# Conditioning blocks of a two-block network on one core: from matmuls and column sums to dot products along turned weight rows on VectorE

## The chip, the core and the metric

The kernel runs on one core of a Trainium2 chip. The metric is device time in microseconds (us), the median of several runs. TensorE is PE in the views (its weight load is PEld), VectorE is DVE, ScalarE is ACT, GpSimd is POOL, SyncE is SP. A name with q (ACTq, SPq) is that engine's instruction queue, where it issues DMAs.

## What is computed

A network of two blocks on 256 tokens of 1024 channels, in float32. Only the first block is touched. Its two layers are conditioned by one vector `c`: six vectors of 1024 per layer (shift, scale and gate of the mixer, shift, scale and gate of the feed-forward), each the product of `silu(c)` with a 1024 x 1024 slice of `w_ada`.

```
def first_block(x, c, w_ada, b_ada, ...):
    sc = jax.nn.silu(c)
    for i in range(DEPTH):
        mod = sc @ w_ada[i] + b_ada[i]
        sh_m, sc_m, g_m, sh_f, sc_f, g_f = jnp.split(mod, 6, axis=-1)
        h = modulate(x, norm_mix[i], sh_m, sc_m)
        ...                       # layer 0: attention; layer 1: gated short convolution
        x = x + g_m[:, None, :] * y
        h = modulate(x, norm_ffn[i], sh_f, sc_f)
        x = x + g_f[:, None, :] * swiglu(h, w_gate_up[i], w_down[i])
    return x
```

The second block (a gated recurrence or stick-breaking attention, memory attention, and a mixture of experts, twice) follows on the same core.

## The kernel before, in words

Weights come in pieces ("units") of [128, 1024] float32, 512 KB each, loaded by SP in an order written out in `make_plan`, into a ring of 34 buffers (`tS`, `raw`, `hi`, `lo` all live there). A "dense" unit is split into two float32r parts before it is multiplied: `hi` by a cast, mostly on ACT (L493), `lo = raw - hi` on DVE (L474). The tokens are two tiles of 128, T0 and T1. Each dense unit is used by both tiles with three matmuls per 128 rows of weights, so 12 matmuls of 512 columns a unit (L439).

The order of instructions on every engine is fixed when the program is built: `Sched` interleaves the parts of the program (tile 0, tile 1, splitting of units, the conditioning `ada_task`) by its own estimates of when each can go on. On the chip each engine then takes its instructions strictly in that order.

A conditioning block (i, j), layer i, vector j, is eight units. j is 0 and 3 for the shifts, 1 and 4 for the scales, 2 and 5 for the gates. In the plan the units of (0, 2) and (0, 4) alternate with units of `qkv`, those of (0, 3) with the eight units of the attention's output weights `wo`, those of (0, 5), (1, 1), (1, 0) and (1, 2) with the first feed-forward, and so on. Before the change there are two ways to work them:

* the five blocks in `ADA_PE`, all of layer 0, are **streamed** through PE: for each half of 512 columns eight matmuls with `silu(c)` as weights (`cs`, 32 columns wide, tile `bk<-raw,cs`), a copy to SBUF, four transposes and a reduction, which leave the vector as columns, one value a partition, in `mcol`;
* the other seven are **summed on DVE** over their eight units, `dst = w * cs[:, k] + dst` (L485, tile `tS<-raw,cs,tS`). The sums over partitions are then made on PE: for shifts and scales by matmuls with a column of ones (`bk<-one,tS`), for gates by splitting the sums and two matmuls of 512 columns with a matrix of ones for each half.

A gate ends as one row, repeated over the partitions, that multiplies the mixer's or the feed-forward's output. Shifts and scales are used by `lhsT_task`: when a tile is normalized (`modnorm`: a square on ACT, L465, a power on POOL, L508, a multiplication on DVE, L479), its halves are transposed on PE, multiplied and shifted by ACT with columns of `mcol` (L471), and split by ACT and DVE. The feed-forward of layer 0 so begins only when `mod0_4` and `mod0_3` are there.

Of the kernel before, what the change touches and what calls it, by code (L numbers as in the profile page):

```python
# [9 lines left out]
F32R = mybir.dt.float32r  # L10
U8 = mybir.dt.uint8
AF = mybir.ActivationFunctionType
# [11 lines left out]
ADA_PE = ((0, 1), (0, 0), (0, 2), (0, 4), (0, 3))  # L24
# [6 lines left out]
# ---------------------------------------------------------------- host layout  # L31
# [28 lines left out]
class Plan:  # L60
    """The order in which pieces of the weights are loaded."""
# [87 lines left out]
def host_arrays(inp):  # L149
# [3 lines left out]
    for i in range(2):  # L153
        for j in range(6):
            w = np.ascontiguousarray(g["w_ada"][i][:, j * D:(j + 1) * D])
            u[f"ada{i}_{j}"] = _split_units(w) if (i, j) in ADA_PE else w.reshape(8, 128, 1024)
# [27 lines left out]
    rows = np.stack([rowsrc[s] for k, (s, i) in zip(plan.kind, plan.src) if k == "row"])  # L184
# [47 lines left out]
# ---------------------------------------------------------------- emission order  # L232
class Sched:
    """Interleaves the parts of the program by an estimate of when each can go on."""
# [54 lines left out]
class Body:  # L289
# [68 lines left out]
    # ---- estimates of when the vector and scalar engines are done  # L358
# [23 lines left out]
    # ---- small helpers  # L382
# [128 lines left out]
    # ---- weights  # L511
# [104 lines left out]
    # ---- pieces  # L616
    def setup(self):
# [30 lines left out]
        self.act(self.cs, self.vecs[:, V_C:V_C + 8], AF.Silu)  # L648

# [20 lines left out]
    def gate(self, i):  # L670
        """Until everything before piece i that is not of its own line has been taken."""
        if i < self.ids["qkv"][6] and not self.again:
            return 0.0
        prev = -1
        for j in range(i - 1, -1, -1):
            if self.plan.kind[j] == "dense":
                prev = j
                break
        return lambda: 0.0 if self.seen >= prev else math.inf

    def ada_task(self):
        for i in range(2):
            order = [(j, (b,)) for b in range(2) for j in (1, 0)] if i == 0 else [(1, (0, 1)), (0, (0, 1))]
            for j, halves in order + [(j, (0, 1)) for j in (2, 4, 3, 5)]:
                uid = self.ids[f"ada{i}_{j}"]
                gate = j in GATES
                onpe = (i, j) in ADA_PE
                dst = None
                if gate or not onpe:
                    yield [self.gate(uid[0]), self.rS(1)]  # L690
                    dst = self.tS()
                if gate:
                    self.nc.gpsimd.memset(dst, 0.0)
                    self.nc.gpsimd.dma_start(dst[0:1, :], self.bada_d[6 * i + j:6 * i + j + 1])
                    yield 4.0
                if not onpe:
                    for k in range(8):
                        yield [self.gate(uid[k]), self.unit(uid[k]), lambda: self.tD - 0.8]
                        w = self.take(uid[k])
                        if k or gate:  # L700
                            self.stt(dst, w, self.cs[:, k:k + 1], dst, ALU.mult, ALU.add)
                        else:
                            self.ts(dst, w, self.cs[:, k:k + 1], None, ALU.mult, None)
                        self.done(uid[k])
                for b in halves:
                    d = dst[:, b * 512:(b + 1) * 512] if dst is not None else None
                    if onpe:
                        yield [self.gate(uid[4 * b + 3]), self.unit(uid[4 * b + 3]), self.bk(1)] + ([] if gate else [self.rH(1)])
                        bank = self.bank()
                        for q in range(4):  # L710
                            raw = self.take(uid[4 * b + q]).rearrange("p (k n) -> p k n", k=2)
                            for kk in range(2):
                                k = 2 * q + kk
                                gq = k % 4
                                self.mm(bank[32 * gq:32 * gq + 32], self.cs[:, k:k + 1].to_broadcast([128, 32]), raw[:, kk], k < 4, k >= 4)
                                self.sch.now -= 0.22
                            self.done(uid[4 * b + q])
                        if gate:
                            self.tt(d, bank, d, ALU.add)
                        else:  # L720
                            d = self.tH()
                            self.scopy(d, bank)
                        self.free()
                    if gate:
                        yield [self.rH(3)]
                        hi, lo = self.tH(F32R), self.tH(F32R)
                        ones = self.ones
                        if onpe:
                            ones = self.tH(F32R)[:, :128]
                            self.vcopy(ones, self.sel4[:, 0:1].to_broadcast([128, 128]))  # L730
                        self.split(hi, lo, d)
                        yield [self.w(), self.bk(1)]
                        bank = self.bank()
                        self.mm(bank, ones, hi, True, False)
                        self.mm(bank, ones, lo, False, True)
                        self.fH(3 if onpe else 2)
                        self.scopy(d, bank)
                    else:
                        yield [self.w(), self.bk(1)]
                        bank = self.bank()  # L740
                        m = self.mcol[:, i, j, 4 * b:4 * b + 4]
                        c = V_BA + 48 * i + 8 * j + 4 * b
                        if onpe:
                            for q in range(4):
                                self.tr(bank[:, q * 128:(q + 1) * 128], d[:, q * 128:(q + 1) * 128])
                            self.fH()
                            self.red(m, bank.rearrange("p (q g e) -> p q g e", q=4, e=32)[:, :, :, 0], ALU.add)
                            self.tt(m, m, self.vecs[:, c:c + 4], ALU.add)
                        else:
                            for q in range(4):  # L750
                                self.mm(bank[:, q:q + 1], d[:, q * 128:(q + 1) * 128], self.one, True, True)
                                self.sch.now += 0.1
                            self.tt(m, bank[:, :4], self.vecs[:, c:c + 4], ALU.add)
                        if j in (1, 4):
                            c = V_NG + 16 * i + (8 if j == 4 else 0) + 4 * b
                            self.stt(m, m, 1.0, self.vecs[:, c:c + 4], ALU.add, ALU.mult)
                        self.sch.ev[f"mod{i}_{j}_{b}"] = self.chain + 0.12
                    self.free()
                if gate:
                    self.mod[i, j] = dst  # L760
                    self.set(f"mod{i}_{j}")
                elif dst is not None:
                    self.fS()
# [1442 lines left out]
```

## Time and profile before

| | |
|---|---|
| median of 3 runs | 1243.78 us (1238.99 to 1245.82) |
| profiled execution, span from first to last instruction | 1241.5 us |
| PE busy in the span | 1185.2 us (95%) |
| DVE busy | 735.7 us (59%) |
| ACT busy | 548.4 us (44%) |
| bytes moved | 301.87 MB, mean 243 GB/s |

The time of the profiled execution outside its span is not given; the median is 2.3 us above the span. Busy time is an average over stages: the last of DVE's conditioning sums starts 655.5 us after the span's start, and everything that is changed lies before it or in the stage that uses it.

### The profile page before, as it was taken

Reading aid. Unit: us, or ns where it says so; the run is one execution under the profiler, and the core shown is the slowest. Engines: PE = TensorE matmul, PEld = TensorE weight load, DVE = VectorE, ACT = ScalarE, POOL = GpSimd, SP = SyncE. Lnnn points to the kernel's source line nnn. Section 1 sums busy time; section 2 is a strip of 40 time slices with the busy share of each in tenths; the row PEclk is TensorE's granted clock in tenths of the full one; section 3 lists DMA queues with packets and bytes.
Section 4 is the critical chain, followed back from the end, with each engine's and each line's share of the span. In section 5 each row is a group of like instructions: output and inputs, shape, how many; then the busy total and the mean of one; then the engine's idle time right before and its main releaser. Section 6 shows DMA issues by size and latency. Waiting matters only on the chain. (4 is left out here: it accounts for less than half of the span.)

```text
span 1241.5 us, 15838 instructions
## 1 busy us (share of the span) xinstructions
PE 1185.2 (95%) x5892; PEld 874.0 (70%) x5892; DVE 735.7 (59%) x1177; ACT 548.4 (44%) x912; POOL 45.2 (4%) x60
## 2 busy tenths in 40 slices
PE   7999999999989999999999999989998999899995
PEld 5777778888867887888887798765443786675432
DVE  4477667766768886555657567773313755564213
ACT  4565564534455556433445845422211566422211
POOL 0021000000000000000000001000000100000001
PEclk9999999999999999999999999989999899889998
DMA  9986768677766765556663323857999332487991
GB/s 378 408 283 231 277 219 294 243 260 268 278 229 234 278 228 174 211 208 208 209 211 106 118 86 125 313 206 279 394 408 360 139 133 101 156 325 288 410 409 42
DMA packets 83540, 301.87 MB, mean 243 GB/s; under 512 B 9408, under 2 KB 9824, under 8 KB 83456
## 3 DMA queue, kind: packets, MB, share of 16 engines
q1 hardware_dynamic: 82224, 298.39, 65.9%
q0 software_dynamic: 944, 2.02, 0.5%
q8 instruction: 48, 0.79, 0.3%
q10 hardware_dynamic: 288, 0.38, 0.1%
q14 instruction: 36, 0.29, 0.1%
HBM read 299.05 MB, written 2.10 MB: 243 GB/s over the span
## 5 line engine op out<-in xcount | busy, mean ns | idle before, releaser
L439 PE MATMUL bk<-hi,tS 128*128 128x512 f32 (+1 forms) x1760 | 585.8, 399 | 13.0 <-ACT hi L493 9.4
L439 PEld LDWEIGHTS bk<-hi,tS 128*128 128x128 f32 x1760 | 332.7, 190 | 88.9 <-ACT hi L493 10.0
L474 DVE TENSOR_TENSOR lo<-raw,hi 128x1024 fp32r<-128x1024 f32 x266 | 316.3, 1220 | 54.3 <-ACT hi L493 53.1
L439 PE MATMUL bk<-lo,tS 128*128 128x512 f32 (+1 forms) x880 | 344.5, 391 | 1.8 <-DVE lo L474 1.8
L493 ACT CAST hi<-raw 128x1024 fp32r<-128x1024 f32 x262 | 262.8, 1048 | 6.6 <-DMA raw<-in_units_dram 6.4
L439 PEld LDWEIGHTS bk<-lo,tS 128*128 128x128 f32 x880 | 167.5, 190 | 34.7 <-DVE lo L474 3.1
L467 ACT ACTIVATE tH<-bk 128x256 f32<-128x256 f32 (+1 forms) x94 | 42.2, 451 | 237.2 <-PE bk L439 237.1
L439 PE MATMUL bk<-hi,tH 128*128 128x512 f32 x384 | 132.8, 396 | 0.0
L439 PE MATMUL bk<-raw,tB 128*64 128x512 f32 x384 | 87.0, 602 | 0.0
L439 PEld LDWEIGHTS bk<-hi,tH 128*128 128x128 f32 x384 | 72.5, 189 | 15.0 <-issue 0.2
L474 DVE TENSOR_TENSOR tS<-bk,tS 128x512 fp32r<-128x512 f32 (+2 forms) x58 | 35.9, 633 | 70.2 <-ACT tS L493 68.9
L439 PE MATMUL bk<-raw,tH 128*64 128x512 f32 x320 | 74.5, 597 | 1.2 <-ACT tH L493 1.2
L439 PE MATMUL bk<-lo,tH 128*128 128x512 f32 x192 | 75.0, 391 | 0.0
L493 ACT CAST tS<-bk 128x512 fp32r<-128x512 f32 (+1 forms) x60 | 31.8, 544 | 92.3 <-PE bk L439 72.5
L485 DVE SCALAR_TENSOR_TENSOR tS<-raw,cs,tS 128x1024 f32<-128x1024 f32 x52 | 66.5, 1278 | 0.2
L439 PE MATMUL bk<-tS 128*128 128x256 f32 (+2 forms) x316 | 62.3, 342 | 0.0
L439 PEld LDWEIGHTS bk<-raw,tB 128*64 128x64 f32 x384 | 26.4, 138 | 49.3 <-issue 46.1
L439 PEld LDWEIGHTS bk<-tS 128*128 128x128 f32 x316 | 50.3, 203 | 11.2 <-issue 6.5
L474 DVE TENSOR_TENSOR tH<-tH,bk 128x256 f32<-128x256 f32 x44 | 18.4, 419 | 63.3 <-ACT tH L467 63.2
L451 PE MATMUL bk<-identr,tH 128*128 128x128 f32 x272 | 47.3, 279 | 8.5 <-DVE tH L474 5.9
L451 PEld LDWEIGHTS bk<-identr,tH 128*128 128x128 f32 x272 | 33.8, 141 | 30.3 <-issue 10.5
L493 ACT CAST tH<-bk 128x256 fp32r<-128x256 f32 (+1 forms) x52 | 18.5, 355 | 79.6 <-PE bk L451 75.5
(189 smaller groups left out, 1037.2 us busy)
## 6 DMA issues: line engine op xcount, KB each, us to landing
raw<-in_units_dram SPq DMA_DIRECT2D x556, 512.0 KB, 5.6
row<-in_rows_dram SPq DMA_DIRECT2D x9, 512.0 KB, 6.4
x<-in_x_dram SPq DMA_DIRECT2D x2, 512.0 KB, 8.8
xsave<-x POOLq DMA_DIRECT2D x2, 512.0 KB, 9.1
out_dram<-x SPq DMA_DIRECT2D x3, 256.0 KB, 2.0
ulv<-in_ulv_dram POOLq DMA_DIRECT2D x1, 576.0 KB, 7.2
cst<-in_consts_dram SPq DMA_DIRECT2D x1, 290.0 KB, 9.7
out_dram<-x ACTq DMA_DIRECT2D x1, 256.0 KB, 2.0
```

The lines of the kernel that those rows point to most:

```text
L439: self.nc.tensor.matmul(out, lhsT, rhs, start=start, stop=stop, skip_group_check=shared)
L451: self.nc.tensor.transpose(out, in_, self.ident)
L467: self.nc.scalar.activation(out, in_, func, scale=scale)
L474: self.nc.vector.tensor_tensor(out, a, b, op)
L485: self.nc.vector.scalar_tensor_tensor(out, a, s, b, op0, op1)
L493: self.nc.scalar.copy(out, a)
```

## The change

Three blocks of layer 0, the first shift, scale and gate, stay streamed. The blocks (0, 4) and (0, 3), and all that DVE summed before, are now **dot products**: the host turns the weights, so that a unit holds 128 output channels as rows, and one instruction on DVE multiplies a unit by `silu(c)`, repeated on every partition (`crow`), and adds along the row into one column of `mcol`. No sum over partitions is left. Gates become rows by eight transposes of the columns. `crow` is loaded and passed through Silu in `setup`.

```
-ADA_PE = ((0, 1), (0, 0), (0, 2), (0, 4), (0, 3))
+ADA_PE = ((0, 1), (0, 0), (0, 2))
...
-            u[f"ada{i}_{j}"] = _split_units(w) if (i, j) in ADA_PE else w.reshape(8, 128, 1024)
+            u[f"ada{i}_{j}"] = _split_units(w) if (i, j) in ADA_PE else np.ascontiguousarray(w.T).reshape(8, 128, 1024)
...
         self.act(self.cs, self.vecs[:, V_C:V_C + 8], AF.Silu)
+        self.crow = self.tS()
+        r = self.rows_d[self.rows_d.shape[0] - 1]
+        nc.scalar.dma_start(self.crow, bass.AP(tensor=r.tensor, offset=r.offset, ap=[[0, 128], [1, 1024]]))
+        self.act(self.crow, self.crow, AF.Silu)
...
+                if (i, j) in ADA_PE:
+                    yield from self.ada_streamed(i, j, halves, uid)
+                else:
+                    yield from self.ada_dots(i, j, uid)
+        self.fS()
...
+    def ada_dots(self, i, j, uid):
+        for b in range(2):
+            for q in range(4 * b, 4 * b + 4):
+                yield [self.gate(uid[q]), self.unit(uid[q]), lambda: self.tD - 0.8]
+                w = self.take(uid[q])
+                self.nc.vector.scalar_tensor_tensor(w, w, 1.0, self.crow, ALU.mult, ALU.mult,
+                                                    accum_out=self.mcol[:, i, j, q:q + 1])
+                self.onD(1024)
+                self.chain = self.tD = self.tD + 0.1
+                self.done(uid[q])
+            self.ada_column(i, j, b)
+            if j not in GATES:
+                self.sch.ev[f"mod{i}_{j}_{b}"] = self.chain + 0.12
+        if j in GATES:
+            yield [self.w(), self.rS(1)]
+            dst = self.tS()
+            for b in range(2):
+                yield self.bk(1)
+                bank = self.bank()
+                for q in range(4):
+                    k = 4 * b + q
+                    self.tr(bank[:, q * 128:(q + 1) * 128], self.mcol[:, i, j, k:k + 1].to_broadcast([128, 128]))
+                self.scopy(dst[:, b * 512:(b + 1) * 512], bank)
+                self.free()
```

`ada_column` adds the bias (and for scales the gain), as before. `ada_streamed` is the old code for the streamed blocks.

**The start, on ACT.** First before the change, then after; `vecs` holds `c` by columns, and `tS<-in_rows` is the load of `crow`.

```order
L626 DMA vecs<-in_vecs_dram 128x234
L457 ACT_TABLE_LOAD
L467 ACTIVATE cs<-vecs 128x8 [waits DMAHW0_49]
L493 CAST tS<-raw 128x1024 [waits DMAHW1_49]
L493 CAST hi<-raw 128x1024 [waits DMAHW2_49]
```

```order
L626 DMA vecs<-in_vecs_dram 128x234
L457 ACT_TABLE_LOAD
L467 ACTIVATE cs<-vecs 128x8 [waits DMAHW0_49]
L651 DMA tS<-in_rows_dram 128x1024
L467 ACTIVATE tS<-tS 128x1024 [waits DMAHW1_49]
L493 CAST tS<-raw 128x1024 [waits DMAHW2_49]
L493 CAST hi<-raw 128x1024 [waits DMAHW3_49]
```

The load of `crow` is issued by ACT behind the wait for `vecs`, and its Silu, which waits for that load, stands ahead of the first casts of weights.

**The turn from the attention's output weights to the feed-forward, on DVE.** `x_82` and `x_83` are the two tiles, L479 is their normalization, and `tS<-tS 128x512` the split of a normalized half. Before the change:

```order
L474 TENSOR_TENSOR tH<-bk,tS 128x512
L474 TENSOR_TENSOR x_83<-x_83,tH 128x512
L474 TENSOR_TENSOR lo<-raw,hi 128x1024 x2
L474 TENSOR_TENSOR tH<-tH,bk 128x256
L481 TENSOR_SCALAR tm<-tm 128x1
L479 TENSOR_SCALAR tS<-x_83,tm 128x1024
L474 TENSOR_TENSOR tH<-bk,tH 128x256
L485 SCALAR_TENSOR_TENSOR tS<-raw,cs,tS 128x1024
L474 TENSOR_TENSOR tS<-tS 128x512 x2
```

After it (L711 are the dots; here they are of block (0, 3)):

```order
L479 TENSOR_SCALAR tS<-x_82,tm 128x1024
L474 TENSOR_TENSOR lo<-raw,hi 128x1024
L481 TENSOR_SCALAR tm<-tm 128x1
L479 TENSOR_SCALAR tS<-x_83,tm 128x1024
L711 SCALAR_TENSOR_TENSOR raw,mcol<-raw,tS 128x1024 x3
L474 TENSOR_TENSOR mcol<-mcol,vecs 128x4
L711 SCALAR_TENSOR_TENSOR raw,mcol<-raw,tS 128x1024
L474 TENSOR_TENSOR tS<-tS 128x512 x2
L711 SCALAR_TENSOR_TENSOR raw,mcol<-raw,tS 128x1024
L474 TENSOR_TENSOR lo<-raw,hi 128x1024 x2
L711 SCALAR_TENSOR_TENSOR raw,mcol<-raw,tS 128x1024 x2
L474 TENSOR_TENSOR mcol<-mcol,vecs 128x4
```

Seven of the eight dots of (0, 3) now stand behind the normalization of both tiles. Before the change nothing of this block was left there, and T0 had been normalized and split 11 rows of DVE ahead of T1.

**The first feed-forward, on PE.** `identr,tH` are the two transposes of a tile's activations, `hi,tH` and `lo,tH` the matmuls with its down weights, `hi,tS` and `lo,tS` those of the gate and up weights. Before, from one of the eleven steps:

```order
L451 MATMUL bk<-identr,tH 128x128 x2
L439 MATMUL bk<-hi,tS 128x512
L439 MATMUL bk<-lo,tS 128x512
L439 MATMUL bk<-hi,tS 128x512 x2
L439 MATMUL bk<-lo,tS 128x512
```

After:

```order
L451 MATMUL bk<-identr,tH 128x128 x2
L439 MATMUL bk<-hi,tH 128x512
L439 MATMUL bk<-lo,tH 128x512
L439 MATMUL bk<-hi,tH 128x512 x2
L439 MATMUL bk<-lo,tH 128x512
L439 MATMUL bk<-hi,tH 128x512
L451 MATMUL bk<-identr,tH 128x128 x2
```

Both tiles now go through the steps side by side; in nine of the eleven the down matmuls of T0 follow right on its own transposes, where twelve or more matmuls of other work stood between.

## Rows read from the trace of the kernel before

**Rows 1.** Page, part 1: engine, busy us (share of the span), instructions.

```profile
PE 1185.2 (95%) x5892; PEld 874.0 (70%) x5892; DVE 735.7 (59%) x1177; ACT 548.4 (44%) x912; POOL 45.2 (4%) x60
```

**Rows 2.** Stretches: PE, PEld, DVE, ACT, POOL busy us (instructions); clock; DMA.

```profile
103.40:154.80 51.40, 51.40 (x316) 38.74 (x315) 35.81 (x61) 27.78 (x54) 5.87 (x5) 1.00 0.73 260
171.50:176.50 5.00, 2.20 (x11) 1.81 (x11) 3.95 (x7) 2.25 (x6) 0.57 (x1) 0.79 0.32 114
180.00:340.00 160.00, 160.00 (x738) 132.06 (x737) 112.82 (x129) 69.71 (x98) 1.50 (x2) 1.00 0.76 266
372.00:465.00 93.00, 89.54 (x427) 73.56 (x426) 78.48 (x124) 50.48 (x79) 0.55 (x1) 1.00 0.70 248
```

**Rows 3.** Timeline of ACT from the start: start us, us, instruction, [idle before <-releaser].

```profile
4.85 0.21 ACT L467 ACTIVATE cs<-vecs 128x8 f32<-128x8 f32 x1 [2.39 <-DMA vecs<-in_vecs_dram]
4.97 1.03 ACT L493 CAST tS<-raw 128x1024 fp32r<-128x1024 f32 x1
...
12.58 1.04 ACT L493 CAST hi<-raw 128x1024 fp32r<-128x1024 f32 x1 [0.23 <-DMA raw<-in_units_dram]
```

**Rows 4.** DMA issues of the first 3 us: KB each, median us to landing.

```profile
vecs<-in_vecs_dram ACTq DMA_DIRECT2D x1, 117.0 KB, 4.1
```

**Rows 5.** Timeline of PE from the start, with a streamed half.

```profile
7.09 0.79 PE L439 MATMUL bk<-hi,tS 128*128 128x512 f32 x1 [7.09 <-ACT hi L493]
...
24.20 1.92 PE L439 MATMUL bk<-raw,cs 128*32 128x512 f32 x16
26.05 0.50 PE L439 MATMUL bk<-hi,tS 128*128 128x512 f32 x1
...
27.55 0.60 PE L451 MATMUL bk<-identr,tH 128*128 128x128 f32 x4
27.90 0.48 PE L439 MATMUL bk<-hi,tS 128*128 128x512 f32 x1
```

**Rows 6.** Timeline of PE at 262 to 268 us: half of a column sum.

```profile
263.87 0.95 PE L439 MATMUL bk<-one,tS 128*128 128x1 f32 x8
264.68 0.48 PE L439 MATMUL bk<-hi,tS 128*128 128x512 f32 x1
```

**Rows 7.** Groups by form: count, busy us, mean ns, idle before.

```profile
L485 DVE SCALAR_TENSOR_TENSOR tS<-raw,cs,tS 128x1024 f32<-128x1024 f32 x52 | 66.5, 1278 | 0.2
L485 DVE SCALAR_TENSOR_TENSOR tS<-x,tS 128x1024 fp32r<-128x1024 f32 x4 | 4.9, 1225 | 2.2 <-ACT tS L467 2.2
L469 ACT ACTIVATION_READ_ACCUMULATOR tH<-bk,tm 128x1 f32 x32 | 6.3, 197 | 0.0
```

**Rows 8.** Timeline of DVE, 100 to 180 us.

```profile
127.22 0.18 DVE L1039 RECIPROCAL tm<-tm 128x4 f32<-128x4 f32 x1 [1.63 <-ACT tH L469]
...
158.06 2.35 DVE L474 TENSOR_TENSOR lo<-raw,hi 128x1024 fp32r<-128x1024 f32 x2
...
169.00 0.69 DVE L474 TENSOR_TENSOR tH<-bk,tS 128x512 f32<-128x512 f32 x1 [1.45 <-PE bk L439]
...
174.02 0.75 DVE L479 TENSOR_SCALAR tS<-x,tm 128x1024 f32<-128x1024 f32 x1 [0.70 <-POOL tm L508]
```

**Rows 9.** Timeline of PE, 170 to 177 us.

```profile
174.92 1.94 PE L451 MATMUL bk<-identr,tS 128*128 128x128 f32 x8 [1.41 <-DVE tS L479]
176.51 0.78 PE L439 MATMUL bk<-hi,tH 128*128 128x512 f32 x1
```

**Rows 10.** Timeline of ACT at the same place.

```profile
176.04 1.50 ACT L471 ACTIVATE tS<-bk,mcol 128x128 f32<-128x128 f32 x4 [2.13 <-PE bk L451]
177.58 0.62 ACT L493 CAST tS<-tS 128x512 fp32r<-128x512 f32 x1
```

**Rows 11.** Timeline of all engines, 193.5 to 195.6 us, in the feed-forward.

```profile
193.82 0.38 PE L451 MATMUL bk<-identr,tH 128*128 128x128 f32 x2
...
194.24 0.37 ACT L493 CAST tH<-bk 128x256 fp32r<-128x256 f32 x1 [1.62 <-PE bk L451]
```

**Rows 12.** PE's waits, 410 to 500 us: total us, times, longest.

```profile
PE bk L439 <- ACT tS L493: 2.5, 2, 1.8
```

More of the change, by code (lines that the diff above doesn't have):

```diff
@@ L183, in host_arrays @@
     rowsrc["row_gn"] = np.concatenate([g["a_gnorm_2"][0], np.zeros(256, np.float32)])
-    rows = np.stack([rowsrc[s] for k, (s, i) in zip(plan.kind, plan.src) if k == "row"])
+    rows = np.stack([rowsrc[s] for k, (s, i) in zip(plan.kind, plan.src) if k == "row"] + [g["c"][0]])
     b_all = np.ascontiguousarray(g["b_ada"].reshape(12, 1024))
@@ L685, in ada_task @@
                 uid = self.ids[f"ada{i}_{j}"]
[L686 to L763, printed above, removed]
+                if (i, j) in ADA_PE:
[3 more added lines that the diff above has]
+        self.fS()
+    def ada_column(self, i, j, b):
+        m = self.mcol[:, i, j, 4 * b:4 * b + 4]
+        c = V_BA + 48 * i + 8 * j + 4 * b
+        self.tt(m, m, self.vecs[:, c:c + 4], ALU.add)
+        if j in (1, 4):
+            c = V_NG + 16 * i + (8 if j == 4 else 0) + 4 * b
+            self.stt(m, m, 1.0, self.vecs[:, c:c + 4], ALU.add, ALU.mult)
@@ new lines, in ada_dots @@
+    def ada_dots(self, i, j, uid):
[22 more added lines that the diff above has]
+                self.free()
+            self.mod[i, j] = dst
+            self.set(f"mod{i}_{j}")
@@ new lines, in ada_streamed @@
+    def ada_streamed(self, i, j, halves, uid):
+        gate = j in GATES
+        dst = None
+        if gate:
+            yield [self.gate(uid[0]), self.rS(1)]
+            dst = self.tS()
+            self.nc.gpsimd.memset(dst, 0.0)
+            self.nc.gpsimd.dma_start(dst[0:1, :], self.bada_d[6 * i + j:6 * i + j + 1])
+            yield 4.0
+        for b in halves:
+            d = dst[:, b * 512:(b + 1) * 512] if gate else None
+            yield [self.gate(uid[4 * b + 3]), self.unit(uid[4 * b + 3]), self.bk(1)] + ([] if gate else [self.rH(1)])
+            bank = self.bank()
+            for q in range(4):
+                raw = self.take(uid[4 * b + q]).rearrange("p (k n) -> p k n", k=2)
+                for kk in range(2):
+                    k = 2 * q + kk
+                    gq = k % 4
+                    self.mm(bank[32 * gq:32 * gq + 32], self.cs[:, k:k + 1].to_broadcast([128, 32]), raw[:, kk], k < 4, k >= 4)
+                    self.sch.now -= 0.22
+                self.done(uid[4 * b + q])
+            if gate:
+                self.tt(d, bank, d, ALU.add)
+            else:
+                d = self.tH()
+                self.scopy(d, bank)
+            self.free()
+            if gate:
+                yield [self.rH(3)]
+                hi, lo = self.tH(F32R), self.tH(F32R)
+                ones = self.tH(F32R)[:, :128]
+                self.vcopy(ones, self.sel4[:, 0:1].to_broadcast([128, 128]))
+                self.split(hi, lo, d)
+                yield [self.w(), self.bk(1)]
+                bank = self.bank()
+                self.mm(bank, ones, hi, True, False)
+                self.mm(bank, ones, lo, False, True)
+                self.fH(3)
+                self.scopy(d, bank)
+            else:
+                yield [self.w(), self.bk(1)]
+                bank = self.bank()
+                for q in range(4):
+                    self.tr(bank[:, q * 128:(q + 1) * 128], d[:, q * 128:(q + 1) * 128])
+                self.fH()
+                self.red(self.mcol[:, i, j, 4 * b:4 * b + 4], bank.rearrange("p (q g e) -> p q g e", q=4, e=32)[:, :, :, 0], ALU.add)
+                self.ada_column(i, j, b)
+                self.sch.ev[f"mod{i}_{j}_{b}"] = self.chain + 0.12
+            self.free()
+        if gate:
+            self.mod[i, j] = dst
+            self.set(f"mod{i}_{j}")
```

## Prediction

> **What bounds the kernel now.** First the page's busy times: PE works in 95% of the span, DVE in 59%, ACT in 44% [rows 1]. The average hides stages, so next the busy time by stretches [rows 2]. In the attention (103.4 to 154.8 us) and in most of the first feed-forward (180 to 340 us) PE is busy for every microsecond, at a granted clock of 1.00, with DMA at 0.73 and 0.76 and DVE at 0.70 of the time. There a matmul taken from PE gives back its time, 160.00 us / 738 = 0.217 us, and work added to DVE is free as long as nobody waits for it. Two places are otherwise. At the turn from the output weights `wo` to the feed-forward (171.5 to 176.5) PE works 2.20 of 5.00 us: it waits for residual, norm and affine. In 372 to 465 us DVE is busy for 78.48 of 93 us, with little room. So the question is not how much DVE gets to do, but what stands behind it at the turn and at the start.
>
> **The change, term by term** (plus is longer).
>
> *The start, +6.0.* Before, ACT gets `vecs` at 4.85 and casts at once, at 4.97 [rows 3]; PE starts at 7.09, behind that work [rows 5]. After, ACT issues the 512 KB load of `crow` only at about 5.0, waits for it, and passes it through Silu, and all first casts are queued behind. The nearest row for the landing is `vecs`: 4.1 us for 117 KB, issued beside the same stream of weight loads [rows 4]. With some 0.9 us for four times the bytes it lands at 10.0; a Silu over 1024 columns costs about what the cast of 1024 does, 1.03 [rows 3]; so the first cast stands at 11.0 instead of 4.97, and PE begins at 13.1. The lower bound is +5 (landing as `vecs` did, 9.1). The upper one is +9 to +10: if the load came in only behind the seven weight loads issued by then, the last of which releases ACT at 12.58 [rows 3], the first cast would be at 13.9. I take the lower half, since `vecs` itself was issued among those loads and was not held back to their end. Nothing gives this back: PE has no gap until 154.8.
>
> The Trainium skill (DMA: Bandwidth & Descriptors, section "Queues, rings and completion order") says that a DMA engine takes turns between the queues it has work for, packet by packet. By that rule ACT's load shares with SP's and the term is +6; by plain order it would be +10. The 4.1 us agree with the rule.
>
> *Streaming of (0, 4) and (0, 3), -9.* A half has a group of matmuls with `cs` from 24.20 to 26.05, 1.85 us, and four transposes from 27.55 to 27.90, 0.35 us [rows 5]: 2.2 us. Four halves are 8.8, with the transposes' own start-up (2.45 a half) 9.8. All lay where PE was full.
>
> *Column sums, -6.5.* Eight matmuls of one column take from 263.87 to 264.68, 0.81 us [rows 6], once for each of the eight halves of (1, 1), (1, 0), (1, 4), (1, 3). Four lie in the full stretch (-3.2 sure); the others lie near the DVE-heavy one, where they may give nothing. That is put into the term for the second layer below.
>
> *Gates of layer 0's feed-forward and layer 1, 0.* Four matmuls of 512 columns (0.9 us) go, eight transposes (0.8 us before they overlap) come.
>
> *One dot, 1.3 us.* No row has a multiplication with a sum along the row on DVE. Nearest: the same instruction without a sum, from two SBUF operands, at 1278 and 1225 ns [rows 7]; ACT's reading of an accumulator costs 197 ns as a separate instruction [rows 7]. So 1.2 to 1.5; I take 1.3. Before, 52 of the same length and four shorter ones were there; now 72. The 16 more that come from the streamed blocks, some 21 us of DVE, stand between 100 and 185 us.
>
> *DVE behind PE in the attention, +1.7.* In 103.4 to 154.8 DVE worked 35.81 us [rows 2], and waited for exponentials as at 127.22 (1.63) [rows 8], four times, some 5 us in all. Three dots join it before the last attention split of T1: 35.8 + 3.9 + 5 = 44.7, while PE without streaming needs 51.4 - 9 = 42.4. Between 0 (the waits shrink when DVE comes later) and +2.5; I take 1.7.
>
> *The turn, +15.7, the largest.* Seven of the eight dots of (0, 3) stand behind the norm of both tiles, and no matmul of the feed-forward can go before them, since ACT adds the shift. Counting from PE's last `wo` matmul: residual of T1 1.3 (twice 0.69, as at 169.00), a `lo` of 1.15 (2.35 for two, at 158.06), T0's norm with its wait for POOL 1.5 (0.70 + 0.75, at 174.02) [rows 8], another `lo` 1.15, T1's norm 1.5, three dots 3.9, the bias 0.2, ACT's affine 1.5 and cast 0.6 [rows 10], and 0.2 between engines: 13.0 us. PE has only eight transposes to do, which cost it 0.8 net; 12.2 idle. If the POOL waits are hidden, 10.8. The second half: a dot, two tile splits (0.7 each, paced by ACT's casts), a dot, two `lo`, two dots, a bias, about 11.5 with its waits, then affine and cast of both tiles, 2.3: 13.8, against 24 matmuls (5.2), transposes and what is left of PE's earlier work (3.1): 5.5 idle. Then the first Silu and the transposes of both tiles, now side by side, 2.0. Together 19.7 us in place of what stands there now: 1.41 before the transposes at 174.92 and the rest up to 176.51 [rows 9], with the 2.13 for which ACT waits at 176.04 [rows 10] inside it, about 4. Now T0's matmuls cover T1's norm; after it both tiles wait for the same dots. The term is +15.7, from +11 (second half fully covered, POOL hidden) to +18.
>
> *The feed-forward side by side, +6.* In nine of eleven steps T0's down matmuls follow on its own transposes. Row: transposes at 193.82, ACT's cast at 194.24 for 0.37, so `hi` is there at 194.61 [rows 11]; 0.8 us after the start, of which the transposes occupy 0.15. 0.65 x 9 = 5.9. It is 0 if DVE and ACT are ahead by then; they are not likely to be, as the cast waits for the transposes themselves.
>
> *Second layer, -2.5.* Now PE waits twice for a cast, 2.5 us in all, on entering the second feed-forward [rows 12]; after, T1 still has matmuls of the mixer left there. Against it stand the column sums' doubtful 3.2. Bounds -3 to +3.
>
> Sum: 6.0 - 9 - 6.5 + 1.7 + 15.7 + 5.9 - 2.5 = +11.3. The profiled span is 1241.5; the median of the runs shown is 1243.8, 2.3 above, and carries over: 1252.8 of span, some 1254.5 of median (rounded down by half a microsecond, since more bounds lie below a term than above).
>
> **Rivals.** *The costs are half hidden, no measurable change.* The waits at the turn are at their lower bound (+11), the lockstep costs 2 instead of 6, the start 5: 5 - 9.5 - 6.5 + 1 + 11 + 2 - 2.5 = +0.5, about 1244. For it: ACT and DVE do have room on average. Against it: the three dots ahead of the first affine stand in a fixed order, and nothing for PE stands beside them.
>
> *Faster: the turn is covered.* One mechanism: PE reaches the end of `wo` later than DVE's queue allows, so that the dots run while `wo` is still multiplied, and the turn costs what it does now. Then 6 - 9 - 6.5 = -9.5, about 1234. It decides when the extra idle at the turn and behind it is under 9.5 us. For it: the units come in early (DMA at 0.73). Against it: the dots stand behind T1's norm, and that behind the last `wo` matmul.
>
> *Dots at half speed.* The nearest row without a sum, 1278 ns, twice, is 2.56 us a dot. Six dots on the path at the turn add 7.7, and some 16 dots in the stretch with 14.5 us of DVE left (372 to 465) add 20 - 14.5 = 6 to 20. About 1254.5 + 7.7 + 13 = 1275. For it no row; against it that the two operands from SBUF alone do not cost double in 1278 ns.
>
> The Trainium skill (Vector Engine (DVE) Microarchitecture Reference, section "7. Points that are easy to get wrong") says that this form with two sources in SBUF that are not bf16 halves its throughput, as no port is left for the accumulator. The rows without accumulator show 1024 elements in 1278 ns; none here shows the form with one.
>
> *The load of `crow` comes last.* The start at +10: 1258.5, inside the forecast's own range.
>
> **How the numbers follow.** The forecast, 1248 to 1262 with its own bounds, has 0.55 (with the late `crow`); half hidden 0.25; the covered turn 0.14; slow dots 0.06. A change of 0.5%, 6.2 us, is about what a measurement can tell here from none. Below 1237.6: most of the covered turn and little else, 0.15. Within: the half-hidden case and the lower edge of the forecast, 0.27. Above 1250: 0.58. The range leaves out the slow dots and the lower half of the covered turn: 1236 to 1267.
>
> **What would show it.** In the changed profile: PE's first matmul at about 13 us; a PE gap of some 12 us ahead of the feed-forward's first matmuls, released by ACT's affine, with three dots and no waits ahead of it on DVE, and a second of some 5; dots at 1.2 to 1.5 us each; small gaps of 0.6 us released by ACT's cast in the first feed-forward; no `one` matmuls. The forecast is wrong if the start is under 10 us, if PE idles less than 12 us in all at the turn, or if the steps run gapless.

## The result, and the profile after

The changed kernel takes 1271.53 us (median of 4 runs, 1270.74 to 1274.44) against 1243.01 us before: ratio 1.0236, 95% interval 1.0209 to 1.0264. It is slower, as forecast, but by 28.5 us where 11 were forecast, and outside the range. The profiled execution has a span of 1270.0 us.

The page's busy times after, beside [rows 1]:

```profile
PE 1178.0 (93%) x5760; PEld 869.3 (68%) x5760; DVE 749.9 (59%) x1261; ACT 545.9 (43%) x905; POOL 39.9 (3%) x54
```

PE's busy time is only 7 us less, not 15 (a matmul at the lower clock counts its longer time), and PE is idle for 92 us instead of 56. To find where, I count on PE's timeline the matmuls of 512 columns with `hi` or `lo` parts of weights, which are the same work in both kernels, and compare when the n-th starts (the first is n = 0). The difference to before, in us:

```
n      place                             before at   after   difference
0      start                                 7.1      15.5     +8.4
300    ahead of the attention              102.0     110.3     +8.4
475    near the end of wo                  164.9     166.9     +2.0
540    behind the turn                     185.4     204.2    +18.8
1200   late in the first feed-forward      344.5     365.9    +21.3
1500   second layer's mixer                431.1     448.1    +17.0
1740   second feed-forward                 495.1     521.0    +25.9
2520   start of the second block           683.6     711.1    +27.6
```

Where the kernels' orders differ, the n-th matmul need not be the same one, so a single row can be off; at the end the difference is 28.5 us. Four places lose: the start, the turn, the entry into the second feed-forward, and a little, 2.6 us, behind n = 1740. Two stretches gain: the attention, where streaming is gone, and the way to the second layer's mixer, where the column sums and some older waits are.

**The start.** ACT's timeline (start, us, instruction, idle before), to be read against [rows 3]:

```profile
5.31 0.21 ACT L467 ACTIVATE cs<-vecs 128x8 f32<-128x8 f32 x1 [2.84 <-DMA vecs<-in_vecs_dram]
...
12.52 1.06 ACT L467 ACTIVATE tS<-tS 128x1024 f32<-128x1024 f32 x1 [7.01 <-DMA tS<-in_rows_dram]
13.49 1.03 ACT L493 CAST tS<-raw 128x1024 fp32r<-128x1024 f32 x1
```

The load of `crow`, issued at 5.31, holds ACT for 7.01 us; the first cast stands at 13.49 instead of 4.97. By the trace's landing times the load was there at 12.50, ahead of two weight loads issued before it (13.06 and 14.32), so the rival that it comes last is out. PE's first row follows:

```profile
15.51 0.79 PE L439 MATMUL bk<-hi,tS 128*128 128x512 f32 x1 [15.51 <-ACT hi L493]
```

**The turn.** PE's timeline from the last `wo` matmul, where before there were the waits of [rows 9]:

```profile
167.81 0.39 PE L439 MATMUL bk<-hi,tS 128*128 128x512 f32 x1
173.52 1.11 PE L451 MATMUL bk<-identr,tS 128*128 128x128 f32 x4 [5.32 <-DVE tS L479]
176.30 1.08 PE L451 MATMUL bk<-identr,tS 128*128 128x128 f32 x4 [1.67 <-DVE tS L479]
182.09 0.79 PE L439 MATMUL bk<-hi,tS 128*128 128x512 f32 x1 [4.70 <-ACT tS L493]
182.68 0.63 PE L439 MATMUL bk<-lo,tS 128*128 128x512 f32 x1
...
193.03 0.80 PE L439 MATMUL bk<-hi,tS 128*128 128x512 f32 x1 [2.57 <-ACT tS L493]
```

The four waits are 14.3 us: two for the norms of T0 and T1, one for the dots with the affine, one for the second half. DVE at the same place, with both norms (L479) ahead of the dots:

```profile
172.71 0.75 DVE L479 TENSOR_SCALAR tS<-x,tm 128x1024 f32<-128x1024 f32 x1 [0.75 <-POOL tm L508]
...
175.40 0.75 DVE L479 TENSOR_SCALAR tS<-x,tm 128x1024 f32<-128x1024 f32 x1 [0.74 <-POOL tm L508]
176.07 1.22 DVE L711 SCALAR_TENSOR_TENSOR raw<-raw,tS 128x1024 f32<-128x1024 f32 x1
177.21 0.08 DVE L711 DVE_READ_ACCUMULATOR raw<-raw,tS 128x1 f32 x1
177.21 1.22 DVE L711 SCALAR_TENSOR_TENSOR raw<-raw,tS 128x1024 f32<-128x1024 f32 x1
```

Behind the waits the matmuls are slow at first. The stretches (PE, PEld, DVE, ACT, POOL busy; then the granted clock):

```profile
170.00:180.00 10.00, 2.20 (x8) 1.43 (x8) 8.44 (x16) 1.74 (x4) 1.13 (x2) 0.61 0.57 206
180.00:190.00 10.00, 7.91 (x30) 6.40 (x31) 7.49 (x11) 5.93 (x12) 0.00 (x0) 0.71 0.41 119
190.00:200.00 10.00, 7.43 (x29) 5.81 (x28) 5.82 (x10) 7.72 (x14) 0.00 (x0) 0.83 0.44 153
```

Eight matmuls from 182.09 to 185.66 take 3.57 us, at the lower of the two clock levels (1.2 instead of 2.4 GHz), where 8 x 0.217 = 1.74 was the pace of [rows 2].

**The dots**, in the groups by form and line:

```profile
L711 DVE SCALAR_TENSOR_TENSOR raw<-raw,tS 128x1024 f32<-128x1024 f32 x72 | 86.9, 1219 | 0.0
L711 DVE DVE_READ_ACCUMULATOR raw<-raw,tS 128x1 f32 x72 | 5.9, 83 | 0.0
```

**The steps of the first feed-forward.** One of nine equal rows on PE, the first matmul of T0's down weights:

```profile
218.61 0.50 PE L439 MATMUL bk<-hi,tH 128*128 128x512 f32 x1 [0.46 <-ACT tH L493]
```

**The entry into the second feed-forward.** PE, and below it DVE, at the end of the second layer's mixer:

```profile
477.66 0.39 PE L439 MATMUL bk<-hi,tS 128*128 128x512 f32 x1
484.19 1.97 PE L451 MATMUL bk<-identr,tS 128*128 128x128 f32 x8 [6.14 <-DVE tS L479]
```

```profile
475.13 4.62 DVE L474 TENSOR_TENSOR lo<-raw,hi 128x1024 fp32r<-128x1024 f32 x4
479.67 0.68 DVE L474 TENSOR_TENSOR tH<-bk,tS 128x512 f32<-128x512 f32 x1
480.39 0.69 DVE L474 TENSOR_TENSOR x<-x,tH 128x512 f32<-128x512 f32 x1
481.00 1.65 DVE L485 SCALAR_TENSOR_TENSOR tB<-tB,vecs 128x127 f32<-128x127 f32 x8
482.57 0.15 DVE L481 TENSOR_SCALAR tm<-tm 128x1 f32<-128x1 f32 x1
483.38 0.75 DVE L479 TENSOR_SCALAR tS<-x,tm 128x1024 f32<-128x1024 f32 x1 [0.66 <-POOL tm L508]
```

PE ends T0's output matmuls at 477.9 and has nothing else: T1's convolution is only being worked on (481.00, and again until 495). As at the turn, the eight matmuls behind the transposes are slow, 3.56 us from 485.81 on, with a granted clock of 0.53 from 484 to 490. Before, T1's output matmuls stood there, T0's transposes followed them without a wait, and the waits were those of [rows 12]:

```profile
469.48 0.39 PE L439 MATMUL bk<-hi,tS 128*128 128x512 f32 x1
469.71 1.04 PE L451 MATMUL bk<-identr,tS 128*128 128x128 f32 x8
472.55 0.50 PE L439 MATMUL bk<-hi,tS 128*128 128x512 f32 x1 [1.80 <-ACT tS L493]
```

### The profile page after: what moved, and what is told of

Same layout as the page of the kernel before. It is cut to its first block, busy times and chain, and to the rows that moved or that the text cites. A ratio compares the mean times of both kernels' runs of the same rounds, so it can differ in the third digit from the quotient of the medians.

```text
span 1270.0 us, 15613 instructions
## 1 busy us (share of the span) xinstructions
PE 1178.0 (93%) x5760; PEld 869.3 (68%) x5760; DVE 749.9 (59%) x1261; ACT 545.9 (43%) x905; POOL 39.9 (3%) x54
## 5 line engine op out<-in xcount | busy, mean ns | idle before, releaser
L474 DVE TENSOR_TENSOR lo<-raw,hi 128x1024 fp32r<-128x1024 f32 x266 | 316.8, 1222 | 65.4 <-ACT hi L493 64.3
L711 DVE SCALAR_TENSOR_TENSOR raw<-raw,tS 128x1024 f32<-128x1024 f32 x72 | 86.9, 1219 | 0.0
L451 PE MATMUL bk<-identr,tH 128*128 128x128 f32 x256 | 44.6, 277 | 11.2 <-DVE tH L474 4.4
L474 DVE TENSOR_TENSOR tH<-bk,tH 128x256 fp32r<-128x256 f32 (+1 forms) x52 | 20.8, 401 | 53.6 <-ACT tH L493 53.6
```

Source lines behind the costliest of these rows:

```text
L451: self.nc.tensor.transpose(out, in_, self.ident)
L474: self.nc.vector.tensor_tensor(out, a, b, op)
L711: self.nc.vector.scalar_tensor_tensor(w, w, 1.0, self.crow, ALU.mult, ALU.mult, accum_out=self.mcol[:, i, j, q:q + 1])
```

## The experiments

The theory after this reading: start, turn and second entry each cost what the table shows. The rivals: that the start is absorbed later; that the second entry only follows from the turn, or from DVE's load; that the turn's cost is the length of the dots, or the order of the tiles. Kernel n is the kernel of experiment n.

**1. `crow` off the start** (e1_crow_late): SP loads it beside `x[1]`.

```
-        nc.scalar.dma_start(self.crow, ...)
-        self.act(self.crow, self.crow, AF.Silu)
+        self.onA(1024)
...
+                self.nc.sync.dma_start(self.crow, ...)
...
+                if (i, j, halves) == (0, 1, (1,)):
+                    self.nc.scalar.activation(self.crow, self.crow, AF.Silu)
```

`onA` keeps the program's estimate of ACT's time as it was.

> The changed kernel with the load of crow issued by SP beside the load of the second tile of tokens, and its Silu on ACT behind the first streamed block instead of ahead of the first casts. If the 8.4 us by which PE starts later are carried to the end, 1271.5 - 8.4 = about 1263, with PE's first matmul near 7 us again. If they are absorbed at a later wait (the turn's dots were late in any case), 1270 to 1272.

Measured: 1264.99 us, ratio 1.0182 (1.0158 to 1.0207). The difference to the changed kernel's ratio is 0.54%, 6.7 us: most of the 8.4 is carried to the end.

**2. (0, 4) and (0, 3) streamed again, the rest dots** (e2_l0_streamed).

```
-ADA_PE = ((0, 1), (0, 0), (0, 2))
+ADA_PE = ((0, 1), (0, 0), (0, 2), (0, 4), (0, 3))
```

> The changed kernel with the blocks (0, 4) and (0, 3) streamed through PE again; (0, 5) and the second layer stay dots, crow stays at the start. If the loss on entering the second feed-forward is made by the second layer's own dots on a full DVE: +8.4 (start) - 6 (column sums) + 9 on 1243 = about 1254, with the wait of some 6 us before the second feed-forward still there. If that loss only follows from the tiles going side by side since the first turn: 1243 + 8.4 - 6 = about 1245, and the wait is gone. In both cases no wait above 2 us at the first turn.

Measured: 1255.5 us, ratio 1.0110 (1.0086 to 1.0135). The difference to before, counted as above, is +8.3 at the start, -1.0 at n = 1500 and +7.5 at n = 1740: everything gained on the way to the second layer is given back at the entry into the second feed-forward, with its wait:

```profile
467.16 1.97 PE L451 MATMUL bk<-identr,tS 128*128 128x128 f32 x8 [5.82 <-DVE tS L479]
```

The wait does not come from the first turn, which is untouched here.

**3. Only (0, 4) and (0, 3) as dots** (e3_l0_dots_only): the kernel before, with

```
+DOTS = ((0, 4), (0, 3))
...
+                if (i, j) in DOTS:
+                    yield from self.ada_dots(i, j, uid)
+                    continue
```

> The kernel before with only the blocks (0, 4) and (0, 3) as dots; (0, 5) and the second layer stay column sums on DVE, crow is at the start. If the second layer's loss is made by its own dots: start 8.4 + turn and lockstep 10 to 14 on 1243 = 1262 to 1266. If it follows from the tiles side by side: 1271 to 1277, with the wait before the second feed-forward there too.

Measured: 1270.69 us, ratio 1.0220 (1.0193 to 1.0246), between the two expectations. The time is nearly that of the changed kernel, but the loss is made up otherwise. The wait of 6 us ahead of the second feed-forward is not there (1.81 is the longest), and the second layer's column sums are not saved (+25.6 at n = 1200, +23.5 at n = 1500). The stretch behind them loses 6 us all the same (+29.4 at n = 1740), in shorter waits and at a lower clock (last section).

**4. The start alone** (e4_start_only): the kernel before with the four lines that make `crow`.

> The kernel before with nothing added but the load of crow and its Silu at the start. If the later start is carried: 1243 + 8.4 = about 1251. If it is absorbed in some later wait of PE: 1243 to 1245.

Measured: 1249.43 us, ratio 1.0059 (1.0036 to 1.0081), 7.3 us. The difference to before is +8.5 at the start and still +8.7 at n = 1740. The start is settled.

**5. Short dots in the second layer** (e5_short_l1_dots), on kernel 2:

```
+                n = 8 if (i, j) in ((1, 4), (1, 3)) else 1024
-                self.nc.vector.scalar_tensor_tensor(w, w, 1.0, self.crow, ...
+                self.nc.vector.scalar_tensor_tensor(w[:, :n], w[:, :n], 1.0, self.crow[:, :n], ...
```

> As e2_l0_streamed, but the 16 dots of (1, 4) and (1, 3) read only 8 of their 1024 columns (so these two vectors lack nearly all of their sum); the order of instructions is the same. It takes some 16 us of DVE out of the second layer's mixer. If DVE sets the entry into the second feed-forward and so gave back the 9 us that PE gained there: 1255.5 - 6 to -9 = 1246 to 1250, and the wait of 5.8 us shrinks to under 2. If the order of the tiles alone makes that wait: 1253 to 1256, with the wait above 4 us.

Measured: 1253.41 us, ratio 1.0084 (1.0061 to 1.0107); the wait is 5.81 us, unchanged. DVE's time on these dots doesn't make it.

**6. Short dots of (0, 3)** (e6_short_turn_dots): the changed kernel, with the same edit and `(i, j) == (0, 3)`.

> As the changed kernel, but the eight dots of (0, 3) read only 8 of their 1024 columns (so this shift lacks nearly all of its sum); the order is the same. If the length of the dots at the turn makes the turn dear: PE's waits of 4.7 and 2.6 us go to under 2.5 together, and with the clock behind them 1271.5 - 7 to -9 = 1263 to 1265. If it is the order (both norms uncovered): the waits of 5.3 and 1.7 us ahead of the transposes stay, and the time is 1268 to 1271.

Measured: 1268.55 us, ratio 1.0213 (1.0192 to 1.0235). The waits at the turn are 5.32, 1.67, 1.52 and 1.81, 4.0 less in sum, and the time is about 3 us lower (the intervals overlap): the dots' length at the turn is the smaller part of its cost.

**7. The units of (0, 3) loaded earlier** (e7_turn_early), on kernel 1:

```
-    weave([("qkv", "dense")] * 12, ada(0, 2) + ada(0, 4))
-    weave([("wo", "dense")] * 8, ada(0, 3))
+    weave([("qkv", "dense")] * 12, ada(0, 2) + ada(0, 4) + ada(0, 3))
+    put("wo", "dense", 8)
```

> As e1_crow_late, but the units of (0, 3) are loaded among those of qkv, ahead of wo, so that their dots lie before the turn. If the dots' place was the turn's cost: PE's idle time at the turn falls from 14 to about 7 us (both norms stay uncovered), 1265 - 7 to -9 = 1256 to 1258. If DVE or the loads become late in the attention instead: 1263 or more, with PE waits between 100 and 165 us above the 3.4 us of now.

Measured: 1268.72 us, ratio 1.0219 (1.0200 to 1.0238), above kernel 1. PE idles 14.7 us at the turn (4.31, 0.47, 7.66, 2.22) and 5.5 us in the attention. The edit moved the loads, but the dots did not come to lie before the turn. DVE behind T1's norm:

```profile
167.25 0.75 DVE L479 TENSOR_SCALAR tS<-x,tm 128x1024 f32<-128x1024 f32 x1 [0.74 <-POOL tm L508]
167.92 1.22 DVE L713 SCALAR_TENSOR_TENSOR raw<-raw,tS 128x1024 f32<-128x1024 f32 x1
...
169.46 1.22 DVE L713 SCALAR_TENSOR_TENSOR raw<-raw,tS 128x1024 f32<-128x1024 f32 x1
```

The last dot of (0, 4), at 167.92, and all eight of (0, 3), from 169.46 on, stand behind both norms, where kernel 1 has seven. So this run does not test the dots' place; it shows that loading the units earlier, in this order, buys nothing.

**8. Kernels 1 and 2 in one** (e8_late_streamed).

> e1_crow_late and e2_l0_streamed in one: crow off the start, (0, 4) and (0, 3) streamed, only (0, 5) and the second layer as dots. If the terms add up: 1255.5 - 7 = 1248 to 1249, still 4 to 7 above the kernel before, by the wait ahead of the second feed-forward and one at the entry to the second block. If the earlier start lets the second layer's units come in late: 1252 or more.

Measured: 1246.99 us, ratio 1.0040 (1.0025 to 1.0055). The terms add up, to within 1 us.

**9. The units of (1, 4) and (1, 3) earlier** (e9_l1_early), on kernel 8:

```
-    weave(ffn(0), ada(0, 5) + ada(1, 1) + ada(1, 0) + ada(1, 2))
-    weave([("win", "dense")] * 24, ada(1, 4) + ada(1, 3))
+    weave(ffn(0), ada(0, 5) + ada(1, 1) + ada(1, 0) + ada(1, 2) + ada(1, 4) + ada(1, 3))
+    put("win", "dense", 24)
```

> e8_late_streamed with the units of (1, 4) and (1, 3) loaded among those of the first feed-forward instead of the second layer's mixer, which also puts all of T1's output matmuls of the mixer beside T0's norm again. If the order of the tiles makes the 9 us given back ahead of the second feed-forward: the wait of 5.8 us goes to under 2, and 1247 - 7 to -9 = 1238 to 1240, about 4 under the kernel before. If not: 1245 to 1248.

Measured: 1233.28 us, ratio 0.9913 (0.9892 to 0.9935): faster than both kernels, and 5 us below what was expected. T0's transposes for the second feed-forward follow without a wait; the longest wait there is 1.81 us, behind them, as before the change. The expectation counted only the 9 us at the entry; the loss in the second block went too (see 15).

**10. Another order at the turn** (e10_turn_order): the changed kernel, where the program's own estimate takes no time for the dots of (0, 4) and (0, 3).

```
-                self.onD(1024)
-                self.chain = self.tD = self.tD + 0.1
+                if i or j == 5:
+                    self.onD(1024)
+                    self.chain = self.tD = self.tD + 0.1
```

> The changed kernel with one thing altered: the program's own estimates, by which the order is laid out, take no time on DVE for the dots of (0, 4) and (0, 3). The work is the same; T0's last wo matmuls, its norm and its first feed-forward matmuls now stand ahead of T1's, as before the change, and the dots of (0, 3) ahead of T0's norm. If the order of the tiles is most of the turn's cost: PE idles 3 to 6 us there instead of 14, the steps' waits of 0.46 us go, and 1271.5 - 11 to -16 = 1256 to 1261. If DVE cannot have the dots done in time (the length of the work is the cost): 1266 to 1272, with PE waiting for the affine at the turn as long as now.

Measured: 1268.69 us, ratio 1.0201 (1.0178 to 1.0224). The turn is cheap, and yet little is won: the time is that of the second expectation, the place is not. PE's waits, and DVE ahead of the first of them:

```profile
144.69 1.65 PE L439 MATMUL bk<-tB 128*128 128x128 f32 x6 [7.24 <-DVE tB L489]
...
164.23 1.09 PE L451 MATMUL bk<-identr,tH 128*128 128x128 f32 x4 [5.28 <-ACT hi L493]
...
179.69 1.09 PE L451 MATMUL bk<-identr,tS 128*128 128x128 f32 x8 [1.30 <-DVE tS L479]
...
191.75 1.94 PE L451 MATMUL bk<-identr,tS 128*128 128x128 f32 x8 [2.77 <-DVE tS L479]
```

```profile
138.98 1.22 DVE L711 SCALAR_TENSOR_TENSOR raw<-raw,tS 128x1024 f32<-128x1024 f32 x1
...
142.41 1.22 DVE L711 SCALAR_TENSOR_TENSOR raw<-raw,tS 128x1024 f32<-128x1024 f32 x1
...
143.95 0.68 DVE L489 COPY tB<-bk 128x512 f32<-128x512 f32 x1
```

Four dots in a row stand on DVE ahead of the copy for which the attention's matmuls wait. The loss has moved from the turn into the attention.

**11 and 12. All corrections with the dots kept** (e11_both_orders: kernel 9 with three blocks in `ADA_PE` and the edit of 10), and the same with the scale's block loaded and worked ahead of the gate's (e12_scale_first).

> All corrections together with the dots kept as in the changed kernel: crow off the start, the estimates of e10_turn_order, the units of (1, 4) and (1, 3) as in e9_l1_early. If the three causes add up: about 1271.5 - 7 (start) - 13 (turn) - 9 (second layer) - 1 to -4 = 1238 to 1242; below e9_l1_early if dots are worth more than streaming in the first layer at all. If DVE is what is short: above e9_l1_early by 5 or more.

> As e11_both_orders, but the scale's block (0, 4) is loaded and worked ahead of the gate's block (0, 2), so that eight dots lie earlier and the streamed gate later. T0's and T1's halves stand closer together at the turn than in e11. By the tiles' order it should lie above e11_both_orders by 2 to 6 us; if only the dots' place counts, below it.

Measured: 1248.99 us, ratio 1.0043 (1.0027 to 1.0059), and 1253.72 us, ratio 1.0085 (1.0064 to 1.0106). Kernel 11 is 15.7 us above kernel 9; they differ by the 16 dots of (0, 4) and (0, 3) in place of streaming and by the order laid out with them. Kernel 12 is another 4.7 us above, within the 2 to 6 us expected. In both, all 16 dots lie ahead of both norms.

**13 and 14. All sixteen dots of (0, 4) and (0, 3) short**, once under the order of 10 (e13_order_short), once under the changed kernel's own (e14_short_l0_dots): the edit of 5 with `i == 0 and j != 5`.

> As e10_turn_order, but the sixteen dots of (0, 4) and (0, 3) read only 8 of their 1024 columns (so these two vectors lack nearly all of their sum); the order is the same. In e10_turn_order the turn was nearly free, yet PE waited 7.2 and 5.3 us in the attention, behind four dots each on DVE. If these waits are DVE's time on dots: both go under 1.5 us and 1268.7 - 15 to -20 = 1249 to 1254. If they come from the loads or from the gate: both stay above 4 us, 1262 or more.

> As the changed kernel, but the same sixteen dots read only 8 of their 1024 columns (so these two vectors lack nearly all of their sum); the order is that of the changed kernel. If DVE's time on dots is all of the cost: 1250 to 1254 as with e13_order_short. If the order of the tiles is a cost of its own: the waits of 5.3 and 1.7 us for the two norms stay, the 0.46 us in nine steps of the feed-forward too, and the time is 1260 to 1266.

Measured: 1251.79 us, ratio 1.0075 (1.0050 to 1.0101), and 1269.92 us, ratio 1.0224 (1.0193 to 1.0255). The second is a miss of both expectations. PE's waits in the attention in kernel 13, where kernel 10 has 7.24 and 5.28:

```profile
143.41 0.63 PE L451 MATMUL bk<-identr,tH 128*128 128x128 f32 x4 [1.00 <-ACT hi L493]
151.12 0.63 PE L451 MATMUL bk<-identr,tH 128*128 128x128 f32 x4 [1.15 <-ACT hi L493]
```

and at the turn in kernel 14:

```profile
173.05 1.11 PE L451 MATMUL bk<-identr,tS 128*128 128x128 f32 x4 [5.32 <-DVE tS L479]
175.82 1.09 PE L451 MATMUL bk<-identr,tS 128*128 128x128 f32 x4 [1.67 <-DVE raw L712]
178.43 0.80 PE L439 MATMUL bk<-hi,tS 128*128 128x512 f32 x1 [1.52 <-ACT tS L493]
```

Under the order of 10, the dots' time is worth 1268.7 - 1251.8 = 17 us (16 by the ratios), nearly all of their 16 x 1.14 = 18. Under the changed kernel's order it is worth 1 to 2 us, which is within the noise: there the order makes nearly all of the loss, since both tiles reach their norms with no matmuls left for PE.

**15. The second layer's order alone** (e15_l1_order): kernel 2, with the estimate of a dot 0.1 us shorter and no other edit.

```
                 self.onD(1024)
-                self.chain = self.tD = self.tD + 0.1
```

> As e2_l0_streamed, but the program's estimate for one dot is 0.1 us shorter (1.14 instead of 1.24 with what it adds for reading the sum). No work differs; in the order that comes out, T1's output matmuls of the second layer's mixer stand beside T0's norm again, as before the change. If that order makes the wait ahead of the second feed-forward: it goes from 5.8 to under 2 us, the small waits at the entry of the second block change too, and the time is 1244 to 1249. If the dots themselves or DVE's load make it: 1253 to 1257.

Measured: 1241.53 us, ratio 1.0003 (0.9987 to 1.0019), 14 us under kernel 2 with the same work (13 by the ratios), and below the 1244 to 1249 expected. PE at the entry:

```profile
469.66 1.06 PE L451 MATMUL bk<-identr,tS 128*128 128x128 f32 x8
472.53 0.69 PE L439 MATMUL bk<-hi,tS 128*128 128x512 f32 x1 [1.81 <-ACT tS L493]
```

Up to n = 1500 it runs as kernel 2 does (-1.1); at n = 1740 the difference to before is +0.6 instead of +7.5, at n = 2520 +0.2 instead of +10.6. So the loss in the second block hangs on that order too; which wait carries it there was not followed. The traces of all runs agree on the entry. Between T0's transposes for the second feed-forward and the mixer's last transposes ahead of them stand 48 matmuls of 512 columns in the changed kernel and in 1, 2, 5, 6, 7, 8, 10, 13 and 14, and T0's transposes wait 4.9 to 6.4 us; 72 to 84 stand there before the change and in all the others, and they do not wait.

**16. Kernel 8 with that estimate** (e16_late_l1_order).

> e8_late_streamed (crow off the start, the first layer's five blocks streamed) with the shorter estimate of e15_l1_order. If start and order add up: 1241.5 - 7 = 1234 to 1236, some 0.6% under the kernel before and equal to e9_l1_early, so that moving the units there was worth nothing beyond the order. If the units' place had a worth of its own: 1237 or more.

Measured: 1233.88 us, ratio 0.9921 (0.9895 to 0.9947), as kernel 9: moving the units was worth nothing beyond the order.

## Why the prediction was wrong, step by step

- **What bounds the kernel** held: PE, with a few places where DVE and ACT stand in front of it.
- **The start, +6.0**: the mechanism was right, the term too small. 8.4 us, in the upper half of its bounds: the load took 7.0 us of ACT's wait where 5 were taken. The 0.9 us added for four times the bytes had no row behind it; from issue to landing `vecs` took 4.5 us and the 512 KB of `crow` 7.2. Kernels 1 and 4 show it carried to the end, to 6.7 and 7.3 us.
- **Streaming -9 and DVE behind PE +1.7**: together -7.3; the difference went from +8.4 to +2.0, that is -6.4.
- **One dot, 1.3 us**: 1.14 from one to the next, and 1219 ns for a dot by itself, no longer than the `lo` subtraction (1222). The rival of dots at half speed is out. The Trainium skill (Vector Engine (DVE) Microarchitecture Reference, section "7. Points that are easy to get wrong") says that this form with two sources in SBUF that are not bf16 halves its throughput; these rows do not agree with it.
- **The turn, +15.7**: the size was right (+16.8), the cause only in part, and the size partly by luck. I had the dots as the path, with both norms as waits ahead of them. Kernels 6 and 14 show that the dots' length is worth 4.0 us of PE's waits there and 1 to 3 us of the time; the rest is that T0 no longer runs ahead of T1, so that no matmul covers either norm, and that PE comes back at the lower clock. PE idles 14.3 us where 12.2 and 5.5 were summed; some 3 us of matmuls at the lower clock (an estimate from the PE rows from 182.09 and 193.03 on, against 0.217 us each), which were in no term, make up for most of it.
- **The rival "the turn is covered"** had its mechanism in kernel 10, and did not win: with the turn covered, the dots stand in the attention's own chain and cost 17 us there. In [rows 2] DVE had 51.4 - 35.8 = 15.6 us left in that stretch, less than 16 dots need (18), and in short waits.
- **The feed-forward +5.9, with the four column sums that lay in it, -3.2**: +2.5 from n = 540 to 1200; nine waits of 0.46 instead of 0.65.
- **The second layer, -2.5: the step that failed.** It said that PE would find T1's mixer matmuls while T0 enters the second feed-forward. The gain on the way there came in full (-4.3 from n = 1200 to 1500), but those matmuls were not ready, T0 entered alone, and +8.9 followed, with another 2.6 behind n = 1740 that no term had. With the other four column sums (-3.3) the forecast had -5.8 from n = 1200 on, and +7.2 was measured. That is 13 of the 17 us missed; the start makes 2.4. Kernels 5 and 15 show that it was neither the dots' time nor DVE's load, but the tiles' order, which a 0.1 us change in the program's estimate turns. I could have read it in the order, where T0's transposes for the feed-forward come 48 matmuls after the mixer's last transposes, and before the change 72.
- **The signs of being wrong** did not come: PE starts at 15.5, idles 14.3 us at the turn, and the steps have their waits. All of them looked at places where the forecast had a loss, none at the entry into the second feed-forward, where it had a gain.

What stays open: whether an order exists in which the 16 dots of (0, 4) and (0, 3) cost less than streaming these blocks. Of the four orders tried none does: kernels 1 and 7 lie 18 and 22 us above kernel 8, kernels 11 and 12 lie 16 and 20 us above kernel 9. Whether the dots' place alone helps under the changed kernel's order was not tested.

## What to carry to other kernels

Work that leaves the bounding engine is free elsewhere only if the other engine has its spare time at the right place in its own queue; compare the spare time of that stretch, not of the kernel, with the work's whole length. Where a program lays out its order by estimates, a change acts through the order as much as through the work: here 0.1 us in one estimate was worth 13 to 14 us, so look at which tile's matmuls stand beside each norm before counting what was saved. And a load that is needed 100 us later belongs behind the first loads and off the engine that the start waits for: with that and the order repaired, the dots of (0, 5) and the second layer alone bring the kernel 0.9% under the one before.

## What was unexpected of the hardware

The clock fell while PE was busy. In kernel 3, after waits of 0.68 and 0.62 us, the stretch from 475 to 485 has PE busy throughout at a granted clock of 0.66; in kernel 4, in a stretch with a longer wait (1.81 us, ahead of 481.21), the clock stays at 1.00. Kernel 3:

```profile
465.00:475.00 10.00, 8.71 (x46) 7.08 (x45) 8.62 (x10) 5.27 (x8) 0.00 (x0) 1.00 0.76 254
475.00:485.00 10.00, 10.00 (x35) 8.05 (x35) 7.67 (x18) 3.46 (x4) 0.00 (x0) 0.66 0.27 92
```

Kernel 4:

```profile
475.00:485.00 10.00, 8.19 (x39) 6.38 (x38) 4.78 (x9) 5.93 (x13) 1.02 (x2) 1.00 0.58 195
```

35 matmuls, column sums included, went where 46 to 50 go at full clock, some 3 us. Kernels 15 and 16 show that the wait's length does not decide it: both wait 0.68 and 0.98 us ahead of the same output matmuls, and in the 10 us behind, with PE busy throughout, the granted clock is 1.00 in kernel 15 (44 matmuls from 450 to 460) and 0.83 in kernel 16 (36 from 443 to 453). Why the short waits cost the clock in one and not in the other, these runs don't show. Reading the accumulator on DVE costs nothing that can be seen: 83 ns, inside the 1.14 us from one dot to the next.
